# Projections for gates, queries, keys and values, emitted as steps inside the latent attention instead of as a block behind it

## The chip, the cores and the metric

The kernel runs on one core of a Trainium2 chip. The metric is the device time of one execution in microseconds (us). The profile is one execution, recorded by the hardware profiler; its times are counted from the first instruction. Engine names are those of the profile: PE is the matrix engine (PEld its weight loads), DVE the vector engine, ACT the scalar engine, POOL the GpSimd engine, SP the engine that issues most DMAs.

## What is computed

Two transformer blocks follow each other on 512 tokens of width 1024 in float32. The first ends in a mixture of sixteen experts; its weights are most of what is read. The change is in the second block, of which this is the core:

```python
h = rmsnorm_2(x, norm_g) * (1 + scale) + shift
ckv, kr, kb, vb, cq, za, qb, zb, ga, gb = split_cols(h @ w_in, KV_SPLITS + Q_SPLITS)
qa, ka, va = latent(cq, ckv, kr)             # 8 heads, 64 + 32 rotary columns, 256 more context rows
oa = block_attention(qa, ka, va, mla_scale)                       # the latent attention
ob = neighborhood_attention(qb, kb, vb, ctx_kb, ctx_vb, rpb)      # the near attention
ya = (oa * silu(za)) @ w_oa
yb = (ob * silu(zb)) @ w_ob
y = (sigmoid(ga) * ya + sigmoid(gb) * yb) @ w_out
x = x + gate * y
```

So the products of `h` with the columns for `za`, `ga`, `gb`, `qb`, `kb` and `vb` need only `h`. The latent attention doesn't need them, and the near attention doesn't need `oa`.

## The kernel before

The kernel is written in a tile framework. A tile names a pool and a tag; the tag has a fixed number of buffers, and a new tile of a tag waits until one is free. The framework places the instructions itself, with a timeline that it computes while it compiles: on each engine, of the instructions that are ready by this timeline, the one that was emitted earlier goes first. The order that results is fixed; on the chip every engine runs its own list from the front, and an instruction that waits holds those behind it.

A product of float32 operands is made from a high and a low part of each operand (`mm3`, lines 133 to 136: three matmuls). Weights come through `WStream` (line 188), one 512 KB block after the other in a fixed order: a DMA on SP, a copy to the high part on ACT (line 233), and the subtraction that gives the low part on DVE or POOL (line 234). There are two buffers for raw blocks (`P3W`) and six for parts (`P3H`), and two blocks, four part buffers, are one pair of 256 output columns.

The work around the change, by its name in the code:

- `latent()` (from line 1674): four pairs of heads, each in two halves of 256 queries, so eight units. A unit has six steps, one for each 128 keys. A step is `scores` (six matmuls and an exponential on ACT, psum tag `sc`), the next piece of `first` for the unit that follows (keys, transposed queries, and `peak`, the score maxima, which DVE reduces from tag `mx`), and `pv` of the step before. A unit ends with `close`: sums, a reciprocal on DVE and the output `oaT`. `first` of the first unit runs ahead of all.
- The projections, called fills below: `gate_fill` (silu gate `za`, letter A: four tiles of psum), `gates` (G10 and G00, two tiles each), `tok_fill` (Q and V, four each) and `keys_b` (K, two). They are called behind `latent()` in the order `MORD` = A G10 Q K G00 V. One tile takes 24 matmuls of 512 columns or 48 of 256. A gate tile leaves psum by a tanh on ACT (line 1657) and a product on DVE (line 1658), for A; the others by ACT alone.
- psum: `MPS` gives `sc` 2 buffers, `mx` 1, `po` 1 and `fl` 1. The fills take the first `NFL` = 5 tiles from `fl`, then `fl`, `sc`, `sc` in turn. Of 18 tiles 10 are `fl` and 8 are `sc`.
- `zaT`, where A's tiles go, is a tile of tag `b8` in pool `p3m`, with three buffers. It is requested behind `latent()`, in which pairs 1 and 3 request their transposed queries `qT` of the same tag.
- Behind the fills: the pools of the latent attention close, and `near()` opens its own. `key_turn` (line 1831 and following) turns the keys, `voff` takes shifted copies of `vb` by DMA (lines 1818 and 1819), and `near()` runs 16 units. Its own fills, `NORD` (more gates, and `out_proj`), are emitted behind it.
- `Filler` (line 285) takes generators and a credit in us: `pull(us)` adds credit and runs steps while it is positive, and each step takes off what it yields.

Of the kernel before, what the change touches and what calls it, by code (L numbers as in the profile page):

```python
# [9 lines left out]
F32 = mybir.dt.float32  # L10
# [3 lines left out]
AF = mybir.ActivationFunctionType  # L14
# [18 lines left out]
P1P=dict(ps=4,pp=2)  # L33
FO=[6,5,7,8,4]
PB2=6
NFL=5
PXE=1
NW_=9
NP=4
# [38 lines left out]
def body(ctx, tc, a, stop=None, dump=None):  # L78
# [44 lines left out]
    def ps(shape=(128, 512), dt=F32, tag="ps"):  # L123
        if tag == "fx":
            tag = next(fills)
        if tag == "tn":
            return ptn.tile(list(shape), dt, name=nm("ps"), tag=tag, bufs=2)
        return PS["pool"].tile(list(shape), dt, name=nm("ps"), tag=tag, bufs=PS[tag])
# [13 lines left out]
    def tsl(t):  # L142
        return slice(t * 128, (t + 1) * 128)
# [248 lines left out]
    def feat_block(w, m, act, p):  # L392
        for k in range(8):
            mm3(p, w(k, tsl(m)), act(k), k == 0, k == 7)
# [1240 lines left out]
    oaT = []  # L1635
    vb = p3m("b8", [128, 4, 512], F32, "vb")

    def tok_fill(x0, dst, scale=1.0, tag="fx"):
        for i in range(2):
            w = w3.pair(x0 + 2 * i)  # L1640
            for t0, nt, p in tok_block(w, 256, hT, tag=tag):
                c = slice(256 * i, 256 * i + 256)
                if isinstance(dst, list):
                    for t in range(nt):
                        S.activation(dst[t0 + t][:, c], p[:, t], AF.Copy, scale=scale)
                else:
                    S.activation(dst[:, t0:t0 + nt, c], p, AF.Copy, scale=scale)
                w3.ahead(x0 + 2 * i + 2 + t0 // 2)

    def gate_fill(x0, z, tag="fl"):  # L1650

        for m in range(4):
            p = ps(tag=tag)
            feat_block(w3.pair(x0 + 2 * (m // 2)), m % 2, hT, p)
            w3.ahead(x0 + m + 2)
            zm = z(m)
            S.activation(zm, p, AF.Tanh, scale=0.5)
            V.scalar_tensor_tensor(zm, zm, 1.0, p, op0=OP.add, op1=OP.mult)
# [3 lines left out]
    def gates(v, tiles, tag):  # L1662

        w = w3.pair(X_G[v])
        sgs[v] = []
        for m in range(2):
            p = ps(tag=tag)
            feat_block(w, m, hT, p)
            w3.ahead(X_G[v] + m + 2)
            g = tiles()  # L1670
            S.activation(g, p, AF.Tanh, scale=0.5)
            sgs[v].append(g)

    def latent():
# [93 lines left out]

        units = [(pr, f) for pr in range(4) for f in range(2)]
        for _ in first(0, 0):  # L1770
            pass
        for n, u in enumerate(units):
            g = first(*units[n + 1]) if n < 7 else iter(())
            for j in range(6):
                scores(*u, j)
                next(g, 0)
                if j:
                    pv(*u, j - 1)
            pv(*u, 5)
            for _ in g:  # L1780
                pass
            close(*u)

    psum(**MPS)
    latent()
    room = iter([x[:, t, 512:] for t in range(4)])
    zaT = p3m("b8", [128, 4, 512], F32, "zT")
    for v in MORD.split():
        if v == "K":
            keys_b(1, X["K"], "fx")  # L1790
        elif v == "Q":
            tok_fill(X["Q"], qb, 0.125)
        elif v == "V":
            tok_fill(X["V"], vb)
        elif v == "A":
            gate_fill(X["A"], lambda m: zaT[:, m], "fx")
        else:
            gates((int(v[1]), int(v[2])), lambda: next(room), "fx")
    for m in range(4):
        G.tensor_mul(oaT[m], oaT[m], zaT[:, m])  # L1800
    if stop == "oa":
# [155 lines left out]
    zbT = []  # L1957
    for v in NORD.split():
        if v == "B":
            gate_fill(X["B"], lambda m: zbT.append(p3m("b3", [128, 512], F32, "zT")) or zbT[m])  # L1960
        elif v[0] == "O":
            out_proj(int(v[1]), 0, "fl")
        else:
            gates((int(v[1]), int(v[2])), lambda: (next(room, None) if v != "G21" else None) or p3m("b2", [128, 512], F32, "sg"), "fl")
    if stop == "ob":
        dump("ob", obT.rearrange("p a b -> p (a b)"))
        for i in range(4):
# [21 lines left out]
    ymT = HL(pf, "b8", 4, 8, 512, "ymT")  # L1989
    for i in range(4):  # L1990
        if i == GI:
            gates((3, 1), lambda: p3m("b3", [128, 512], F32, "sg"), "pp")
        out_proj(i, 1, "pp")
        sg = sgs[i, 0] + sgs[i, 1]
        for m in range(2):
            G.tensor_add(sg[m], sg[m], sg[2 + m])
            src = sg[m].rearrange("p (b r c) -> p b r c", r=8, c=8)
            d = [v.rearrange("p (r b c) -> p b r c", r=8, c=8) for v in ymT(2 * i + m)]
            evac_hl(d[0], d[1], src)
        if i == 1:  # L2000
            nc.sync.dma_start(x, xd)
# [148 lines left out]
```

## Time and profile before

| What | us |
| --- | --- |
| median of three runs | 1945.97 (1945.35 to 1950.58) |
| the profiled execution | 1938.7 |
| its span, first to last instruction | 1936.9 |
| latent attention, from its first fill tile to its last sums | 1446 to 1604 |
| fills alone on PE | 1604 to 1675 |
| near attention with its fills | 1675 to 1843 |
| end of the block | 1843 to 1937 |

In the views below a busy time is the sum of an engine's instructions; PE's matmuls overlap, so neighbours in the list start sooner than the busy time of one says. PEclk is the granted clock of PE as a share of the full 2.4 GHz, so that 0.50 is 1.2 GHz. A bracket behind a row of the timeline is the time for which the engine stood idle before it, and what ended that.

### The profile page before, as it was taken

To read this page: it belongs to the slowest core of one execution; us is meant where nothing else is said; L and a number is where in the kernel's file an instruction comes from. 1 tells how busy PE (TensorE), PEld (TensorE's weight loads), DVE (VectorE), ACT (ScalarE), POOL (GpSimd) and SP (SyncE) were. 2 spreads that over 40 slices of the span, in tenths; PEclk is the share of its full clock that TensorE was granted. 3 is DMA by queue.
4 is the path that set the end of the run, shared out by engine and by line. 5 is a ranking of instruction groups with operands and counts; after the bars stand their busy time and mean duration, and the time that the engine had idled before them with its cause. 6 is when DMAs were issued, how large, how long until landed. Compare 5 with 4: busy or idle time off the path is not lost.

```text
span 1936.9 us, 24224 instructions
## 1 busy us (share of the span) xinstructions
PE 1751.3 (90%) x10016; PEld 1066.7 (55%) x10016; DVE 699.8 (36%) x1404; ACT 480.3 (25%) x929; POOL 246.6 (13%) x275
## 2 busy tenths in 40 slices
PE   6998999989999888988989888888899999999998
PEld 5984579963343232422323233322585669888878
DVE  6696786540111101001020010200556642354565
ACT  4335534421000000000000000000653432344433
POOL 2371201000000000000000000000031113223351
PEclk9999999999999999999999999999998999999999
DMA  6323513559999999999999999999420023432232
GB/s 213 109 80 103 190 51 98 206 230 420 425 426 426 426 425 427 426 426 426 426 426 426 426 425 426 425 427 425 144 81 12 1 66 96 103 99 81 87 109 88
DMA packets 96334, 500.47 MB, mean 258 GB/s; under 512 B 6628, under 2 KB 56640, under 8 KB 67808
## 3 DMA queue, kind: packets, MB, share of 16 engines
q1 hardware_dynamic: 90656, 479.06, 62.1%
q0 software_dynamic: 3696, 12.98, 2.0%
q10 hardware_dynamic: 1872, 6.88, 0.9%
q8 instruction: 79, 1.29, 0.3%
q14 instruction: 31, 0.25, 0.0%
HBM read 491.13 MB, written 6.72 MB: 257 GB/s over the span
## 4 chain that ended last, share of the span: by engine, by line
PE 48%; DMA 39%; DVE 6%; ACT 3%; POOL 2%; issue 2%; SPq 0%; DVEq 0%; ACTq 0%; POOLq 0%
DMA we<-in_expert_w_dram 37%; PE ps L131 24%; PE ps L134 7%; PE ps L135 7%; PE ps L136 7%; DMA w<-in_ca_wkv_dram 1%; DMA w<-in_w_out_dram 1%; DVE wl L234 1%; PE ps L1902 1%; ACT wh L233 1%; PE ps L752 1%; POOL wl L234 1%; DVE qkc L530 1%; DMA voff<-vb 1%; POOL sq L462 0%
## 5 line engine op out<-in xcount | busy, mean ns | idle before, releaser
L131 PE MATMUL ps<-we,xe 128*64 128x512 f32 x2048 | 464.8, 602 | 59.6 <-DMA we<-in_expert_w_dram 59.6
L131 PEld LDWEIGHTS ps<-we,xe 128*64 128x64 f32 x2048 | 144.3, 138 | 354.7 <-issue 263.7
L131 PE MATMUL ps<-we,hT 128*64 128x512 f32 x1024 | 233.2, 598 | 28.2 <-DMA we<-in_expert_w_dram 21.6
L131 PEld LDWEIGHTS ps<-we,hT 128*64 128x64 f32 x1024 | 69.8, 136 | 161.5 <-issue 128.3
L233 ACT ACTIVATE wh<-w 128x1024 fp32r<-128x1024 f32 (+4 forms) x100 | 104.0, 1042 | 141.9 <-PE ps L135 94.2
L1307 DVE TENSOR_TENSOR hid<-hid,ps 128x512 f32<-128x512 f32 x32 | 22.0, 688 | 321.8 <-PE ps L131 300.4
L1349 DVE SCALAR_TENSOR_TENSOR y<-ps,gate,y 64x512 fp32r<-64x512 f32 x32 | 24.0, 749 | 311.6 <-ACT y L1348 311.6
L1315 ACT ACTIVATE hT<-ps 128x512 f32<-128x512 f32 x32 | 19.1, 597 | 424.3 <-PE ps L1313 424.3
L305 POOL DMA_DIRECT2D gg<-in_rows_dram x2 | 1.1, 548 | 903.9 <-PE ps L131 903.9
L234 DVE TENSOR_TENSOR wl<-w,wh 128x1024 fp32r<-128x1024 f32 (+4 forms) x62 | 82.5, 1333 | 90.4 <-ACT wh L233 90.1
L234 POOL TENSOR_TENSOR wl<-w,wh 128x1024 fp32r<-128x1024 f32 (+1 forms) x34 | 81.9, 2413 | 198.0 <-ACT wh L233 197.9
L1348 ACT ACTIVATE y<-ps,gate 64x512 fp32r<-64x512 f32 x32 | 21.8, 682 | 259.3 <-PE ps L131 246.2
L134 PE MATMUL ps<-hTh,wh 128*128 128x512 f32 x192 | 76.5, 399 | 1.7 <-ACT va L1631 1.7
L135 PE MATMUL ps<-hTl,wh 128*128 128x512 f32 x192 | 76.0, 396 | 0.0
L136 PE MATMUL ps<-hTh,wl 128*128 128x512 f32 x192 | 75.8, 397 | 0.0
L131 PEld LDWEIGHTS ps<-otT,xn 128*128 128x128 f32 x512 | 60.7, 195 | 24.0 <-issue 21.9
L131 PE MATMUL ps<-otT,xn 128*128 128x128 f32 x512 | 66.3, 285 | 1.0 <-ACT otT L1254 1.0
L135 PE MATMUL ps<-wl,hTh 128*128 128x256 f32 (+1 forms) x224 | 66.2, 296 | 0.0
L134 PE MATMUL ps<-wh,hTh 128*128 128x256 f32 (+1 forms) x224 | 66.2, 297 | 0.0
L136 PE MATMUL ps<-wh,hTl 128*128 128x256 f32 (+1 forms) x224 | 64.9, 295 | 0.0
L1266 DVE TENSOR_TENSOR xe<-ps,cols 128x512 f32<-128x512 f32 (+1 forms) x18 | 10.2, 599 | 145.9 <-PE ps L131 145.9
L1306 ACT ACTIVATE hid<-ps 128x512 f32<-128x512 f32 x32 | 19.1, 596 | 158.7 <-PE ps L131 158.7
(571 smaller groups left out, 3330.6 us busy)
## 6 DMA issues: line engine op xcount, KB each, us to landing
we<-in_expert_w_dram SPq DMA_DIRECT2D x171, 2048.0 KB, 34.3
we<-in_expert_w_dram SPq DMA_DIRECT2D x42, 1024.0 KB, 34.3
w<-in_w_in_dram SPq DMA_DIRECT2D x48, 512.0 KB, 3.7
w<-in_w_mod_dram SPq DMA_DIRECT2D x24, 512.0 KB, 4.3
w<-in_w_out_dram SPq DMA_DIRECT2D x16, 512.0 KB, 3.7
w<-in_ca_wkv_dram SPq DMA_DIRECT2D x8, 512.0 KB, 4.3
wcv<-in_ctx_kv_dram SPq DMA_DIRECT2D x2, 2048.0 KB, 21.7
bm<-in_bias_dram POOLq DMA_DIRECT2D x16, 256.0 KB, 3.0
```

The source lines that it names most:

```text
L131: T.matmul(out, l, r, start=st, stop=sp)
L134: T.matmul(out, L[0], R[0], start=st, stop=False)
L135: T.matmul(out, L[0], R[1], start=False, stop=False)
L136: T.matmul(out, L[1], R[0], start=False, stop=sp)
L233: S.activation(h, w, AF.Copy)
L234: (G if (self.ns % 3 == 2 if self is ws else W3E(self.ns)) else V).tensor_sub(l, w, h.bitcast(F32))
L530: V.scalar_tensor_tensor(o, u[:, 6 + j:518 + j], conv(m, j), o, op0=OP.mult, op1=OP.add)
L752: T.transpose(pp[:, j], st[u][hf][:, tsl(j)], ident)
L1307: V.tensor_mul(h, h, pu)
L1348: S.activation(Y[q][r, 2 * d], p[r], AF.Copy, scale=g)
L1349: V.scalar_tensor_tensor(Y[q][r, 2 * d + 1], p[r], g, Y[q][r, 2 * d].bitcast(F32), op0=OP.mult, op1=OP.subtract)
L1902: T.transpose(p[:, j], st[u][i][:, tsl(j)], ident)
```

## The change

The fills become generators. `tok_part` yields after every four of a tile's k (12 matmuls of 256 columns), `feat_part` after every two (6 of 512 columns), each time 1.4. K is now a case of `tok_fill`. They are handed to a `Filler` before `latent()` starts; `first` of the first unit pulls `FS` = 1.5 after each of its pieces, every step of a unit pulls `FJ` = 2.0 behind its scores, and what is left is drained behind `latent()`. `zaT` is requested before `latent()`. `NFL` becomes 14. The same functions, used behind the near attention, are run to their end at once by `steps_of`.

```diff
-NFL=5
+NFL=14
+FS=1.5
+FJ=2.0
...
+    def tok_part(w, p, t, n):
+        for k in range(8):
+            mm3(p[:, n:n + 256], hT(k, tsl(t)), w(k), k == 0, k == 7)
+            if k % 4 == 3:
+                yield 1.4
+
+    def feat_part(w, m, p):
+        for k in range(8):
+            mm3(p, w(k, tsl(m)), hT(k), k == 0, k == 7)
+            if k % 2:
+                yield 1.4
...
+    def tok_fill(x0, dst, scale=1.0, n=2):
+        for i in range(n):
             w = w3.pair(x0 + 2 * i)
+            for t in (0, 2):
+                p = ps(tag="fx")
+                for j in range(2):
+                    yield from tok_part(w, p, t + j, 256 * j)
+                for d, s in dst(i, t, p.rearrange("p (t n) -> p t n", t=2)):
+                    S.activation(d, s, AF.Copy, scale=scale)
+                w3.ahead(x0 + 2 * i + 2 + t // 2)
...
         for _ in first(0, 0):
-            pass
+            fill.pull(FS)
         for n, u in enumerate(units):
             g = first(*units[n + 1]) if n < 7 else iter(())
             for j in range(6):
                 scores(*u, j)
+                fill.pull(FJ)
                 next(g, 0)
                 if j:
                     pv(*u, j - 1)
             pv(*u, 5)
             for _ in g:
-                pass
+                fill.pull(1)
             close(*u)
...
     psum(**MPS)
-    latent()
     room = iter([x[:, t, 512:] for t in range(4)])
     zaT = p3m("b8", [128, 4, 512], F32, "zT")
...
+    fill = Filler(*(fills_of(v) for v in MORD.split()))
+    latent()
+    fill.drain()
```

## Rows read from the trace of the kernel before

**Rows 1.** The page's first part: busy time, share of the span, instructions.
```profile
PE 1751.3 (90%) x10016; PEld 1066.7 (55%) x10016; DVE 699.8 (36%) x1404; ACT 480.3 (25%) x929; POOL 246.6 (13%) x275
```

**Rows 2.** Busy times by stage; stretch, length, engines (instructions), PEclk, DMA share, GB/s.
```profile
1444.00:1452.00 8.00, 6.34 (x32) 5.02 (x31) 3.90 (x8) 2.88 (x6) 7.56 (x8) 1.00 0.08 26
1452.00:1460.00 8.00, 4.71 (x19) 2.43 (x18) 4.90 (x7) 1.45 (x4) 3.93 (x5) 0.79 0.24 66
1460.00:1475.00 15.00, 15.00 (x59) 9.69 (x59) 5.65 (x8) 5.25 (x9) 0.00 (x0) 0.54 0.00 0
1475.00:1517.00 42.00, 40.43 (x267) 25.66 (x268) 33.94 (x48) 18.64 (x36) 8.00 (x9) 1.00 0.00 1
1517.00:1528.00 11.00, 8.96 (x42) 5.96 (x38) 6.28 (x9) 2.67 (x5) 3.25 (x4) 0.70 0.01 1
1528.00:1542.00 14.00, 13.41 (x89) 8.48 (x86) 11.08 (x16) 7.24 (x15) 1.27 (x1) 0.99 0.01 2
1542.00:1555.00 13.00, 13.00 (x70) 8.47 (x70) 5.83 (x9) 4.21 (x7) 3.50 (x3) 1.00 0.27 86
1555.00:1563.00 8.00, 5.13 (x19) 3.79 (x18) 5.91 (x7) 1.43 (x3) 1.28 (x1) 0.79 0.41 122
1563.00:1604.00 41.00, 40.12 (x224) 28.09 (x223) 16.26 (x20) 12.63 (x19) 3.64 (x2) 1.00 0.09 26
1604.00:1675.00 71.00, 71.00 (x548) 68.91 (x548) 15.16 (x22) 23.67 (x37) 23.05 (x16) 1.00 0.36 99
1675.00:1703.00 28.00, 26.27 (x140) 22.01 (x139) 15.87 (x24) 11.73 (x20) 6.96 (x6) 1.00 0.47 113
1703.00:1843.00 140.00, 139.78 (x930) 112.41 (x930) 70.40 (x127) 60.04 (x123) 47.53 (x47) 1.00 0.29 89
```

**Rows 3.** PE's timeline, 1445 to 1456: start, length, line, operation, idle time before.
```profile
1445.93 0.50 PE L134 MATMUL ps<-hTh,wh 128*128 128x512 f32 x1 [1.66 <-ACT va L1631]
...
1451.52 0.40 PE L136 MATMUL ps<-hTh,wl 128*128 128x512 f32 x1
...
1453.64 0.59 PE L131 MATMUL ps<-kT,qT 96*128 96x512 f32 x2 [1.14 <-POOL kT L1689]
...
1455.37 0.59 PE L131 MATMUL ps<-kT,qT 96*128 96x512 f32 x2 [1.14 <-DVE mx L1710]
```

**Rows 4.** ACT's and DVE's timelines where A's first tile leaves psum.
```profile
1538.74 0.59 ACT L1657 ACTIVATE zT<-ps 128x512 f32<-128x512 f32 x1
...
1536.93 1.76 DVE L1752 RECIPROCAL rs<-ps 128x256 f32<-128x256 f32 x1 [0.19 <-PE ps L131]
...
1539.85 0.67 DVE L1658 SCALAR_TENSOR_TENSOR zT<-zT,ps 128x512 f32<-128x512 f32 x1
```

**Rows 5.** PE's timeline from A's second tile to its third.
```profile
1542.68 0.39 PE L134 MATMUL ps<-hTh,wh 128*128 128x512 f32 x1
...
1553.72 0.40 PE L136 MATMUL ps<-hTh,wl 128*128 128x512 f32 x1
...
1558.76 0.38 PE L131 MATMUL ps<-cst,mx 128*2 128x128 f32 x2 [2.87 <-DVE mx L1710]
...
1559.88 0.63 PE L134 MATMUL ps<-hTh,wh 128*128 128x512 f32 x1
```

**Rows 6.** DVE's timeline in the gap between those two tiles.
```profile
1556.15 1.75 DVE L1752 RECIPROCAL rs<-ps 128x256 f32<-128x256 f32 x1
...
1558.63 0.67 DVE L1658 SCALAR_TENSOR_TENSOR zT<-zT,ps 128x512 f32<-128x512 f32 x1
```

**Rows 7.** DVE's timeline where the latent attention ends and the near one prepares.
```profile
1603.88 1.76 DVE L1752 RECIPROCAL rs<-ps 128x256 f32<-128x256 f32 x1 [0.74 <-PE ps L131]
...
1609.49 1.43 DVE L1831 COPY tk<-x 128x512 f32<-128x512 f32 x4
```

**Rows 8.** The chain that ended last, 1676 to 1687: start, length, what.
```profile
1676.55 10.01 DMA voff<-vb
```

**Rows 9.** PE's timeline, 1675 to 1703, its only idle time over 0.2 us.
```profile
1689.39 1.27 PE L1834 MATMUL ps<-cst,tk 128*128 128x128 f32 x8 [1.73 <-DVE kc L1836]
```

More of the change, by code (lines that the diff above doesn't have):

```diff
@@ L1636, in body, with steps_of @@
     vb = p3m("b8", [128, 4, 512], F32, "vb")
-    def tok_fill(x0, dst, scale=1.0, tag="fx"):
-        for i in range(2):
-            w = w3.pair(x0 + 2 * i)
[L1641 to L1648, printed above, removed]
+    def steps_of(gen):
+        for _ in gen:
+            pass
+    def tok_part(w, p, t, n):
[10 more added lines that the diff above has]
+        for i in range(n):
+            w = w3.pair(x0 + 2 * i)
+            for t in (0, 2):
[5 more added lines that the diff above has]
+                w3.ahead(x0 + 2 * i + 2 + t // 2)
     def gate_fill(x0, z, tag="fl"):
         for m in range(4):
+            w = w3.pair(x0 + 2 * (m // 2))
             p = ps(tag=tag)
-            feat_block(w3.pair(x0 + 2 * (m // 2)), m % 2, hT, p)
+            yield from feat_part(w, m % 2, p)
             w3.ahead(x0 + m + 2)
@@ L1667, in gates @@
             p = ps(tag=tag)
-            feat_block(w, m, hT, p)
+            yield from feat_part(w, m, p)
             w3.ahead(X_G[v] + m + 2)
@@ L1780, in latent, with fills_of @@
             for _ in g:
-                pass
+                fill.pull(1)
             close(*u)
     psum(**MPS)
-    latent()
     room = iter([x[:, t, 512:] for t in range(4)])
     zaT = p3m("b8", [128, 4, 512], F32, "zT")
-    for v in MORD.split():
+    def fills_of(v):
         if v == "K":
[L1790 to L1798, printed above, removed]
+            return tok_fill(X["K"], lambda i, t, p: [(kb[:, t:t + 2, 4:8], p.rearrange("p t (h d) -> p t h d", h=4))], n=1)
+        if v == "Q":
+            return tok_fill(X["Q"], lambda i, t, p: [(qb[t + j][:, 256 * i:256 * i + 256], p[:, j]) for j in range(2)],
+                            0.125)
+        if v == "V":
+            return tok_fill(X["V"], lambda i, t, p: [(vb[:, t:t + 2, 256 * i:256 * i + 256], p)])
+        if v == "A":
+            return gate_fill(X["A"], lambda m: zaT[:, m], "fx")
+        return gates((int(v[1]), int(v[2])), lambda: next(room), "fx")
+    fill = Filler(*(fills_of(v) for v in MORD.split()))
+    latent()
+    fill.drain()
     for m in range(4):
@@ L1959, in body @@
         if v == "B":
-            gate_fill(X["B"], lambda m: zbT.append(p3m("b3", [128, 512], F32, "zT")) or zbT[m])
+            steps_of(gate_fill(X["B"], lambda m: zbT.append(p3m("b3", [128, 512], F32, "zT")) or zbT[m]))
         elif v[0] == "O":
@@ L1963, in body @@
         else:
-            gates((int(v[1]), int(v[2])), lambda: (next(room, None) if v != "G21" else None) or p3m("b2", [128, 512], F32, "sg"), "fl")
+            steps_of(gates((int(v[1]), int(v[2])), lambda: (next(room, None) if v != "G21" else None) or p3m("b2", [128, 512], F32, "sg"), "fl"))
     if stop == "ob":
@@ L1991, in body @@
         if i == GI:
-            gates((3, 1), lambda: p3m("b3", [128, 512], F32, "sg"), "pp")
+            steps_of(gates((3, 1), lambda: p3m("b3", [128, 512], F32, "sg"), "pp"))
         out_proj(i, 1, "pp")
```

## The prediction, made before the changed kernel ran

> **What bounds the kernel now.** I read the page's first part first: PE is busy for 1751.3 us, 90% of the span, and no other engine passes 36% [rows 1]. So the kernel as a whole is paced by PE and, in the experts, by what PE waits for there; the change touches neither the experts nor the number of matmuls. What it can win is time in which PE stands still or runs at the low clock, in the stretch that it rearranges. That is why the second view is the table by stage [rows 2]: for each stretch the reader takes length minus PE's busy time (idle), and length times (1 minus PEclk) (lost to the clock).
>
> Idle, from 1444 to 1604: 1.66 + 3.29 + 0 + 1.57 + 2.04 + 0.59 + 0 + 2.87 + 0.88 = 12.9 us. Clock: 0.21 x 8 = 1.7, 0.46 x 15 = 6.9, 0.30 x 11 = 3.3, 0.01 x 14 = 0.1, 0.21 x 8 = 1.7, together 13.7 us; some of it falls on idle time (the idle shares of the three stretches that have both give 0.7 + 0.6 + 0.6), so 11.8 us count. From 1604 to 1675 PE is busy without a gap, from 1675 to 1703 it loses 1.7, from 1703 to 1843 only 0.2 [rows 2]. **The ceiling of the change is therefore 12.9 + 11.8 + 1.7 = 26.4 us**, 1.4% of the span; the 71 us of fills alone are no waste, since PE does useful work there.
>
> The third view, the timelines, says why the loss sits where it does. The planner already moves fills into the latent attention, and one can see it: A's first tile runs from 1445.93 to 1451.9, inside the preparation of the first unit [rows 3]. Then nothing follows for 87 us. Its tanh runs at 1538.74 [rows 4], though its matmuls were done at 1451.9 and ACT is busy for only 18.64 of 42 us [rows 2]. I read this as a wait for `zaT`: it is the last of the `b8` tiles requested, behind the `qT` of pairs 1 and 3, and pair 1 has just made its last sums (the reciprocal at 1536.93 is its) [rows 4]. While the tile waits, the one `fl` bank is taken and no fill can start. At 1542.68 the second tile starts [rows 5], and from there to 1604 fills and attention alternate. So the latent attention runs alone from 1452 to 1542, with DVE busy for 33.94 of 42 us [rows 2], and there PE has its low clock and most of its gaps.
>
> **The change, part by part.** *Instructions.* None is added or removed on any engine: the same 18 tiles, 8 weight pairs and evictions, so 0 us of work. *Weights.* Their DMAs on SP, the copies on ACT and the subtractions on DVE and POOL move with the fills. SP has nothing else here (DMA share 0.00 to 0.01 from 1460 to 1542), ACT and POOL have room; on DVE they meet a busy engine, but a step that now also holds 2 us of fill lasts about twice as long, so DVE's share falls from 0.81 towards half [rows 2]. I cost it at nothing; without that cover each subtraction on DVE would be one more queue ahead of a maximum, as in the gap below.
>
> *Credit.* `first` pulls 5 x 1.5, the 48 steps pull 48 x 2.0, together 103.5; the 18 tiles yield 18 x 5.6 = 100.8. So the last fill, V, ends in the last but one step of the last unit, and nothing is left to drain. The yield of 5.6 a tile fits: 12 tiles take 71 us with some transposes among them [rows 2].
>
> *`zaT` first.* It now takes a `b8` buffer before `qT` of pair 1, and `qT` of pair 3 has to wait for pair 1 instead, which has ended two units before it is wanted. Cost 0; the 87 us for which a bank was held are gone.
>
> *Start, 1444 to 1460.* Idle now 1.66 + 3.29 = 4.95. The 1.66 (the bank is freed by an eviction on ACT) and the 1.14 before 1453.64 (POOL) [rows 3] stay; the gaps at the maxima are filled by A's second tile, once the first has left psum. I keep 3.0 idle, a gain of 2.0; bounds 0 and 3.3. The low clock follows these gaps: 4.71 busy of 8, then 0.54 for 15 us, while 1.73 idle in 28 us [rows 9] and 0.88 in 41 left it at 1.00 [rows 2]. With the gaps halved I take it as not falling: gain 1.0 + 6.9 = 7.9, rounded to 8, bounds 0 and 8.
>
> *The seven and a half units that follow, 1475 to 1604.* Lost now: idle 7.95, clock 3.9 (of the 11.8), together 11.9. What the interleaved regime loses is shown by its own rows, and they lie apart: 0.88 in 41 us, or, with the gap at 1558.76 and its clock, 2.87 + 0.88 + 1.1 = 4.9 in 62 us (1542 to 1604) [rows 2]. The regime will last about 200 us: the attention's own work is 160 us (1444 to 1604) less the 24.7 lost and less six tiles of fills at 5.6, so 102, and the fills are 101. That gives 4.3 or 15.8 us. The gap arises because a maximum stands behind a 1.75 us reciprocal and a subtraction on DVE [rows 5, 6], when the planner has put the maxima at the seam of two units; with a fill behind every score they have time to come in their own steps. I take 7, nearer to the first: gain 5, bounds -4 and 8.
>
> *The single bank.* 16 of 18 tiles now share `fl`, instead of 10. A tile's bank was free again only 2.0 to 5.8 us after its last matmul (from 1554.1 to 1559.88 in [rows 5], with its DVE product at 1558.63 [rows 6]), and PE must have attention work for that long. It has about 102/18 = 5.7 us for each tile, with two banks for scores, so I cost it at 0 beyond the term above; the third rival has the other end.
>
> *Start of the near attention.* What the 71 us of fills covered comes to stand bare: from the last reciprocal to the end of the key copies 1603.88 to 1610.92, 7.0 us on DVE [rows 7]. What covers it now are the first two tiles of the next gates, 11.2 us of PE, but only if their psum is free. The 10.01 us DMA from `vb` [rows 8] and the gap of 1.73 that comes with it [rows 9] stay late in any order, or come some us sooner, since V ends a step before the attention. Extra cost between -1.7 and 7.0; I take 3, nearer to the covered end. The stretch from 1703 on is full and keeps its length [rows 2].
>
> Sum: 2 + 8 + 5 - 3 = 12 us. The profiled execution would go from 1936.9 to 1925 of span; the median lies 7.3 above the profiled execution's 1938.7 and keeps that distance, so 1946 - 12 = **1934 us**.
>
> **Rivals.** *First, the clock still falls at the start and the near attention starts bare:* 2 + 0 + 5 - 7 = 0 to 2 + 0 + 5 - 3 = 4, so 1942 to 1946. For it: the bank of the first tile and POOL's copies are not touched by the change, and 1517 to 1528 shows a fall after only 2.04 us idle [rows 2].
>
> *Second, nearly all comes back:* 3.3 + 8 + 8 + 1.7 = 21, so 1925. For it: 41 us of the same regime with 0.88 idle [rows 2].
>
> *Third, slower: the bank sets the pace.* PE's list is in order, so a fill placed by the planner before its bank is really free stops scores too. One such turn cost 2.87 + 1.1 = 4.0 us at 1555 to 1563 [rows 2, 5]. Against a ceiling of 26.4 with 3 left at the start and 3 added at the near one, five bad turns of 16 leave nothing of the gain that can be measured; at nine it is 36 - 20 = 16 slower, 1962. Against it: of four turns in 1542 to 1604 one was bad.
>
> The Trainium skill, "TensorE: Matmul & The Clock Gate", section "A second HAM failure mode: psum-queue depth-cycling", speaks against this change: cycling through psum banks makes PE idle briefly between groups of matmuls, often enough that its clock swings between its levels. By that rule this third rival would be the likely one; the trace agrees only once, with PEclk 0.79 at 1555 to 1563, and shows 1.00 over the next 41 us.
>
> *Fourth, the change does not do what it says:* only the move of `zaT` and the planner matter, and steps by hand give what the planner would have given. The time would be that of the forecast, 1934, and its chance lies inside the forecast's; it is a question of cause.
>
> **How the numbers follow.** Chances: forecast 0.46 (1928 to 1938), second rival 0.16, first rival 0.25, third 0.13. A measurement of this kernel can tell about 0.3%, 5.8 us, from no change. Forecast and second rival are faster, 0.62; the first is within, 0.25; the third is slower, 0.13. The range goes from 1922 (the ceiling less 2) to 1950, 4 above the first rival, for the units' term nearer to its lower bound; the third rival and a little on either side stay out.
>
> **What would show it.** Right: A's first tanh within 5 us of its last matmul; no stretch of 0.5 clock between 1455 and 1475; fill matmuls between the scores of all eight units; V's last eviction at the last unit; the first near scores some 10 us sooner than at 1703. Wrong: PE idle ended by ACT or by DVE's `zT` at the turns of the tiles (third rival); PE idle of over 5 us behind the last sums (first); a clock below 1.00 at the seams of the units.

## The result and the profile after

The changed kernel takes **1919.28 us** (median of 4 runs, 1918.83 to 1920.45), the kernel before 1945.66 us in the same measurement (4 runs, 1944.06 to 1950.58). The ratio is 0.9861, with a 95% interval of 0.9843 to 0.9879: 1.4% faster, 26.4 us where 12 were forecast. Its profiled execution took 1919.15 us, its span is 1917.4 us. Against the profiled execution of before, span to span, that is 19.5 us. So the missed 14.4 us are two misses of about the same size: 7.5 in the sum, and 6.9 in the distance between the profiled execution and the median.

The page's first part of the changed kernel; PE was busy for 1751.3 us before [rows 1].

```profile
PE 1739.1 (91%) x10016; PEld 1062.0 (55%) x10016; DVE 702.1 (37%) x1404; ACT 478.4 (25%) x929; POOL 248.0 (13%) x275
```

The number of matmuls is the same, and PE is busy for 12.2 us less: it did the same work at the high clock for longer. The table by stage of the changed kernel (stretch, length, busy time of PE, PEld, DVE, ACT and POOL with the number of instructions, PEclk, DMA share, GB/s), to be held against [rows 2]:

```profile
1444.00:1452.00 8.00, 8.00 (x39) 6.56 (x38) 6.14 (x12) 4.36 (x8) 7.61 (x13) 1.00 0.25 68
1452.00:1465.00 13.00, 11.09 (x51) 7.53 (x50) 6.51 (x11) 4.37 (x8) 8.55 (x7) 1.00 0.30 81
1465.00:1512.00 47.00, 46.19 (x254) 32.75 (x253) 26.52 (x33) 17.45 (x29) 4.17 (x3) 1.00 0.17 45
1512.00:1530.00 18.00, 17.65 (x128) 14.46 (x127) 8.84 (x14) 7.14 (x15) 5.50 (x5) 1.00 0.11 30
1530.00:1654.00 124.00, 123.69 (x877) 98.75 (x875) 57.37 (x72) 45.76 (x78) 25.17 (x17) 1.00 0.21 60
1654.00:1692.00 38.00, 36.15 (x186) 30.47 (x185) 27.91 (x45) 14.34 (x26) 14.14 (x15) 0.96 0.39 101
1692.00:1823.00 131.00, 131.00 (x878) 105.81 (x876) 66.32 (x121) 58.09 (x120) 49.53 (x46) 1.00 0.29 87
```

Length minus PE's busy time gives 0 + 1.91 + 0.81 + 0.35 + 0.31 + 1.85 + 0 = 5.2 us idle, and only one stretch has a clock below 1.00: 0.04 x 36.15 = 1.4 us. That is 6.7 us lost where before lost 26.4 by the same reading. PE's timeline has only seven places from 1444 to 1823 at which it waited for 0.25 us or more (start, length, operation, in brackets the idle time before it and what ended it); the last row is one of the slower matmuls behind the seventh:

```profile
1454.05 0.59 PE L133 MATMUL ps<-kT,qT 96*128 96x512 f32 x2 [1.14 <-DVE mx L1730]
1461.69 0.61 PE L133 MATMUL ps<-kT,qT 96*128 96x512 f32 x2 [0.39 <-DVE mx L1730]
1463.48 0.38 PE L133 MATMUL ps<-cst,mx 128*2 128x128 f32 x2 [0.25 <-DVE mx L1730]
1490.48 0.65 PE L133 MATMUL ps<-P,va 128*64 128x256 f32 x4 [0.32 <-ACT P L1752]
1511.90 0.38 PE L133 MATMUL ps<-cst,mx 128*2 128x128 f32 x2 [0.49 <-DVE mx L1730]
1512.63 0.39 PE L136 MATMUL ps<-wh,hTh 128*128 128x256 f32 x1 [0.35 <-ACT x L1691]
...
1656.04 0.50 PE L136 MATMUL ps<-hTh,wh 128*128 128x512 f32 x1 [1.85 <-DVE rs L1772]
...
1657.20 0.63 PE L137 MATMUL ps<-hTl,wh 128*128 128x512 f32 x1
```

The largest wait has moved to the end: the near attention's first gate tile waits for the last reciprocal, and behind that wait the matmuls of 512 columns take 0.63 us instead of 0.40, the half clock, until 1660.2. ACT's timeline answers [rows 4]: the tanh of A's first tile runs half a microsecond after the start of the tile's last matmul (1451.94), not 87 us later; V's last eviction and the first exponential of the near attention follow.

```profile
1452.42 0.60 ACT L1677 ACTIVATE zT<-ps 128x512 f32<-128x512 f32 x1 [0.83 <-PE ps L138]
...
1646.33 0.59 ACT L1666 ACTIVATE vb<-ps 128x512 f32<-128x512 f32 x1
...
1691.72 0.69 ACT L1918 ACTIVATE P<-ps,mx 128x512 f32<-128x512 f32 x1 [4.57 <-DVE mx L1916]
```

In the kernel before the first of these exponentials ran at 1704.30: 12.6 us of the gain are there by then, and the other 5.5 by the near attention's last output, because 22 of its stretch's matmuls now stand ahead of it.

### The profile page after: what moved, and what is told of

The parts are those of the page before. It is cut to its first block, busy times and chain, and to the rows that moved or that the text cites. A ratio compares the mean times of both kernels' runs of the same rounds, so it can differ in the third digit from the quotient of the medians.

```text
span 1917.4 us, 24223 instructions
## 1 busy us (share of the span) xinstructions
PE 1739.1 (91%) x10016; PEld 1062.0 (55%) x10016; DVE 702.1 (37%) x1404; ACT 478.4 (25%) x929; POOL 248.0 (13%) x275
## 4 chain that ended last, share of the span: by engine, by line
PE 52%; DMA 39%; DVE 5%; ACT 2%; issue 1%; POOL 1%; SPq 0%; ACTq 0%; DVEq 0%; POOLq 0%
DMA we<-in_expert_w_dram 37%; PE ps L133 24%; PE ps L136 8%; PE ps L137 8%; PE ps L138 8%; DMA w<-in_ca_wkv_dram 1%; PE ps L1927 1%; PE ps L754 1%; DVE wl L236 1%; DVE qkc L532 1%; DMA w<-in_w_out_dram 1%; POOL sq L464 0%; ACT wh L235 0%; PE ps L1503 0%; PE ps L260 0%
```

## The experiments

Five questions: what frees the tiles, whether one bank is enough, what it costs the attention to stand alone, what could still be had at the start of the near attention, and why the median moved further than the profile. "Lost" is idle time of PE plus its busy time times (1 minus PEclk), in the stretch named. The runs were made in five groups, each with the kernel before on the same chip. The times are medians; the ratio is taken from all executions of both kernels and not from the two medians, whose quotient would be 0.9912 for e9 and 0.9905 for e10.

| run | us | before beside it | ratio (95%) |
|---|---|---|---|
| e1, before again | 1945.92 | 1942.55 | 0.9997 (0.9974 to 1.0021) |
| e2, steps, nothing pulled | 1953.43 | 1942.55 | 1.0059 (1.0034 to 1.0084) |
| e3, `zaT` touched, 5 in `fl` | 1935.48 | 1942.55 | 0.9954 (0.9926 to 0.9982) |
| e4, `zaT` touched, 14 in `fl` | 1925.19 | 1942.55 | 0.9914 (0.9890 to 0.9938) |
| e5, after again | 1920.62 | 1945.22 | 0.9872 (0.9855 to 0.9888) |
| e6, after, banks shared | 1919.71 | 1945.22 | 0.9868 (0.9851 to 0.9884) |
| e7, after, fills in 4 units | 1918.66 | 1945.22 | 0.9864 (0.9848 to 0.9881) |
| e8, after, V ahead of G00 | 1923.57 | 1945.22 | 0.9883 (0.9867 to 0.9900) |
| e9, after, fills in 2 units | 1924.37 | 1941.44 | 0.9881 (0.9817 to 0.9944) |
| e10, after, one tile left over | 1922.90 | 1941.44 | 0.9867 (0.9804 to 0.9930) |
| e11, before, close late | 1944.12 | 1943.22 | 1.0028 (1.0006 to 1.0049) |
| e12, e3 with close late | 1928.22 | 1943.22 | 0.9926 (0.9900 to 0.9952) |
| e13, after, third time | 1919.37 | 1944.64 | 0.9873 (0.9848 to 0.9898) |
| e14, e4 again | 1925.20 | 1944.64 | 0.9902 (0.9879 to 0.9925) |

### What frees the tiles

The prediction read the 87 us for which A's first tile held the one `fl` bank as a wait for pair 1's end. The lists that the framework makes say something else: with the request of `zaT` alone moved ahead of `latent()`, they are the same as those of the kernel before, so that would be the same kernel. A tile of `b8` gets its buffer in the order of the instructions that first *write* the tag's tiles. In the kernel before the tanh that first writes `zaT` is emitted behind all of the attention, so it stands behind the first write of pair 3's `qT`. ACT's timeline of the kernel before shows just these two, one behind the other:

```profile
1538.48 0.37 ACT L139 ACTIVATE qT<-ps 96x256 fp32r<-96x256 f32 x1
1538.74 0.59 ACT L1657 ACTIVATE zT<-ps 128x512 f32<-128x512 f32 x1
```

(The reciprocal at 1536.93 in [rows 4], which the prediction gave to pair 1, is the fifth unit's, pair 2's first half.) Three kernels tell the readings apart. The first is the changed kernel with nothing pulled, so that the request stands early and the steps are all emitted behind the attention:

```diff
-FS=1.5
-FJ=2.0
+FS=0
+FJ=0
```

> The changed kernel with both credits 0: the fills are generators, zaT is requested first and 14 tiles go to fl, but all steps are drained behind the attention. If the request of zaT is what frees the fills, as the prediction had it: 1920 to 1935. If zaT gets its buffer only by the order in which instructions first write the tiles of its tag, nothing is freed (PE's list then has one fill tile up to the fifth unit's sums, as the kernel before): 1943 to 1949. Both say that the number of fl tiles alone does nothing.

The other two are the kernel before with `zaT` requested and one column of it written ahead of `latent()`, without any steps; e4 has `NFL=14` as well, as the changed kernel has.

```diff
 psum(**MPS)
+zaT = p3m("b8", [128, 4, 512], F32, "zT")
+V.memset(zaT[:, 0, 0:1], 0.0)
 latent()
 room = iter([x[:, t, 512:] for t in range(4)])
-zaT = p3m("b8", [128, 4, 512], F32, "zT")
```

> The kernel before, its fills in one piece behind the attention and 5 tiles in fl, but zaT is requested ahead of the attention and written there by one memset of one column. If the order of first writes is what held A's first tile, the planner now moves fills by itself: its list for PE has 3.8 tiles at the first unit's sums, 6.2 at the third's, and then none until the attention's end, since the next tiles want sc. The losses of the start and of the first three units go (start 3 + 8, a third of the units' 12), the others stay: 1930 to 1934. If emission between the steps is what counts, 1943 to 1949.

> As the last, with 14 tiles in fl. No fill is emitted between steps; the planner's list has 3.8, 5.0, 7.0, 8.4, 10.0, 11.0, 13.8 and 15.0 tiles at the eight units' sums and three behind the attention. If the hold by zaT and the wait for sc are the whole cause, it takes what the change takes, 1917 to 1922, and the three tiles left cover the start of the near attention. If emission in steps has a worth of its own, 1925 to 1940.

With the request early and nothing pulled the hold is there as before: the first tile's last matmul starts at 1456.76, and its tanh runs at 1543.98, again right behind a `qT`. The single write takes it away: in e3 the tanh runs at 1457.07. ACT's timelines of e2 and of e3:

```profile
1543.72 0.37 ACT L141 ACTIVATE qT<-ps 96x256 fp32r<-96x256 f32 x1
1543.98 0.59 ACT L1677 ACTIVATE zT<-ps 128x512 f32<-128x512 f32 x1
```

```profile
1457.07 0.60 ACT L1657 ACTIVATE zT<-ps 128x512 f32<-128x512 f32 x1 [0.83 <-PE ps L136]
```

So the first write is the cause of the hold, shown by taking it away. e2 at 1953.43 us lies above both of its ranges, slower than the kernel before, and its timeline says where: PE idles for 9.9 us from the last sums to the near attention's first exponential, where e1, the kernel before, idles for 1.7. Behind the attention the fills run bare, now through one bank, and six tiles wait for the one ahead of them to be evicted, with idle times of 1.40, 0.75, 1.35, 0.53, 1.40 and 0.69 us (two more waits, 1.08 and 0.60, are for weights). Two of the six:

```profile
1611.60 0.39 PE L136 MATMUL ps<-wh,hTh 128*128 128x256 f32 x1 [1.40 <-ACT x L1691]
...
1625.96 0.39 PE L136 MATMUL ps<-wh,hTh 128*128 128x256 f32 x1 [1.35 <-ACT qb L1666]
```

That is the third rival's mechanism, with its price: 6.1 us for six turns where nothing else stands between two tiles.

How far does one column written early go? In e3 six tiles are made early, and then the tiles of tag `sc` wait for the attention's scores to end. In e4 15 of 18 come early, and the ratio is 0.9914. e3's 1935.48 us lies 1.5 above its range, and e4's 1925.19 at the near end of the range for steps with a worth of their own. Run beside the changed kernel on one chip, in more executions:

> The touched kernel with 14 tiles in the fl bank, unaltered (zaT touched ahead of the attention, no steps), now beside the changed kernel on one chip. In profiled executions it stood 3.6 us above the changed kernel between the attention's start and the near attention's last output, with as little idle. Theory (the steps are worth those 3.6 us, and the rest of the distance between the two ratios, 0.9914 to 0.9867, was the chip's): 3 to 5.5 us slower than the changed kernel. Rival (the steps are worth the whole distance): 7 to 11 us slower.

e14 takes 1925.20 us (6 runs, 1920.42 to 1929.72) and e13, the changed kernel, 1919.37: 5.8 us apart, between the theory's 3 to 5.5 and the rival's 7 to 11, and nearer to the theory. So by the medians, of 25.3 us beside the kernel before, 19.4 come from letting the planner move the tiles, with one write and `NFL`, and about 6 from the steps. The windows of e14 (the first unit, then the other seven) show that the units have nothing left to win: 0.18 us idle in 152 us, at full clock.

```profile
1444.00:1486.73 42.73, 39.31 (x193) 27.37 (x194) 21.76 (x33) 16.01 (x27) 13.46 (x13) 1.00 0.14 39
1486.73:1639.05 152.32, 152.14 (x995) 114.74 (x996) 77.65 (x99) 55.34 (x97) 32.89 (x24) 1.00 0.17 49
```

From the first fill tile to the near attention's last output, the profiled executions take 378.3 us (after), 381.9 (e4) and 379.9 (e14). What e14's other executions lose to the changed kernel's is not settled.

### Is one bank enough?

The changed kernel with only the first 5 tiles kept to `fl`, the others in `fl`, `sc`, `sc` in turn:

```diff
-NFL=14
+NFL=5
```

> The changed kernel with only the first 5 of its 18 filling tiles in the fl bank, the others in the two banks of the scores, as before the change. The third rival of the prediction (the one fl bank sets the pace in the changed kernel): the tiles get a second bank, and it is faster than the changed kernel by 3 us or more. Theory now (the change wins because the filling never stops, and the one bank is hidden by the attention's work between two steps): no faster; a half-made tile now holds a score bank through some ten steps, which leaves the attention one bank for its scores, so 3 to 20 us slower than the changed kernel, with idle of TensorE ahead of score matmuls.

1919.71 us, 0.9 less than the changed kernel on that chip; the executions overlap (1918.37 to 1920.97, and 1919.91 to 1921.35). Neither expectation was right: the third rival's 3 us are not there, nor is the loss of 3 to 20 us to half-made tiles in score banks. The near attention's start loses less in e6 (0.65 and 0.49 us idle in place of 1.85, the clock at 1.00), and the stretch as a whole no less: 378.7 us by the same reading as above. Banks don't set the pace here, in either division.

### What does it cost the attention to stand alone?

The first theory behind the result was that the attention loses time wherever nothing stands between its steps. e7 and e9 are the changed kernel with more pulled at each step, so that all tiles are made beside the first four units, or the first two:

```diff
-FJ=2.0
+FJ=4.0
```

> The changed kernel with twice as much pulled at each of the attention's steps (FJ 4 in place of 2): the same instructions, but all 18 tiles are made by the end of the fourth of eight units and the last four units stand alone. Theory (what the change gives back is lost wherever attention stands alone: in the kernel before 1512 to 1604, which is mostly the last four units, TensorE idled 6.4 us and the clock cost about 4): 8 to 14 us slower than the changed kernel, the idle and the half clock now in the last four units, none of it in the first four. Rival (it is the start of the attention alone, with the clock's fall there, and the order of the first writes that cost): as fast as the changed kernel within 3 us.

```diff
-FJ=2.0
+FJ=8.0
```

> The changed kernel with 8 pulled at each step (FJ 8 in place of 2): all 18 filling tiles are made beside the first two units, and six units stand alone, among them every later change of pair. Theory now (attention that stands alone costs only 0.3 to 0.8 us a unit, as in units 2 to 4 of the kernel before; what is dear is a single place, where DVE's list has the reciprocal of one unit right ahead of the maxima mx that the next unit's queries wait for: TensorE waits 1.9 us there and its clock falls for 3 to 9 us' worth; before has this at the end of unit 4, the touched kernel with 5 tiles at the end of unit 6): this kernel's list has that order at the ends of units 3, 5 and 6, all alone now, so waits of 1.9 us at two or three of them and at least one fall of the clock, 5 to 14 us slower than the changed kernel (1924 to 1933 beside 1919 to 1921). Rival (only the start of the attention mattered; with 18 tiles made early enough nothing is lost later): within 3 us of the changed kernel.

e7 is as fast as the changed kernel (1918.66 beside 1920.62, with ratios whose intervals overlap): the theory fell. The windows of e7, first unit, units 2 to 4 with the fills, and units 5 to 8 alone:

```profile
1444.00:1484.46 40.46, 38.56 (x198) 27.94 (x196) 21.50 (x32) 17.07 (x27) 14.62 (x14) 1.00 0.18 51
1484.46:1602.91 118.45, 118.45 (x831) 100.72 (x830) 45.55 (x55) 40.02 (x66) 27.65 (x17) 1.00 0.23 65
1602.91:1651.76 48.85, 46.27 (x305) 29.51 (x304) 35.80 (x50) 21.15 (x39) 7.63 (x8) 1.00 0.09 31
```

Four units alone lose 2.6 us, and the clock stays. In e9 it is six units, and the loss is the same 2.6; the 4.1 us of idle in its second unit, which holds 14 tiles, are mostly two waits of 1.05 for maxima, one of 1.08 and one of 0.60 for weights, and one of 0.33 at the bank. e9 lies at the near end of its range of 1924 to 1933, but not for the reason given there: no wait of 1.9 us, and no fall of the clock in the units. The windows of e9, its second unit and units 3 to 8:

```profile
1486.59:1588.20 101.61, 97.49 (x681) 86.30 (x680) 25.06 (x32) 30.60 (x50) 20.77 (x14) 1.00 0.24 69
1588.20:1658.00 69.80, 67.22 (x454) 44.45 (x454) 53.97 (x72) 30.27 (x56) 12.86 (x12) 1.00 0.10 31
```

e3, with units 4 to 8 alone, is another matter. Its sixth unit ends with the order that cost the kernel before 2.04 us at 1517 to 1528 [rows 2]: reciprocal, then the maximum for which PE waits. There PE idles 1.90 us and the clock falls to 0.67 for a unit, 2.4 and 6.1 us lost:

```profile
1571.01:1592.01 21.00, 18.62 (x83) 11.50 (x84) 10.33 (x14) 5.15 (x9) 1.26 (x1) 0.67 0.08 31
```

But the same order on DVE stands at three seams of e9 (1599.87, 1624.35, 1636.33) and costs nothing there. DVE and PE at the seam of the kernel before at 1517.64, then at the first of those three in e9:

```profile
1517.64 1.76 DVE L1752 RECIPROCAL rs<-ps 128x256 f32<-128x256 f32 x1 [0.19 <-PE ps L131]
1519.31 0.90 DVE L1710 TENSOR_REDUCE mx<-ps 128x1 f32<-128x768 f32 x1
1520.27 0.38 PE L131 MATMUL ps<-cst,mx 128*2 128x128 f32 x2 [1.90 <-DVE mx L1710]
```

```profile
1599.87 1.74 DVE L1772 RECIPROCAL rs<-ps 128x256 f32<-128x256 f32 x1
1601.53 0.89 DVE L1730 TENSOR_REDUCE mx<-ps 128x1 f32<-128x768 f32 x1
1601.26 2.66 PE L133 MATMUL ps<-qT,kT 98*128 98x256 f32 x18
1603.85 0.38 PE L133 MATMUL ps<-cst,mx 128*2 128x128 f32 x2
```

In e9 PE's list has 18 score matmuls, 2.66 us, ahead of the matmuls that need the maximum; in the kernel before it has nothing there. In the changed kernel two seams have the order as well: at 1611.22 fill matmuls run until 1614.94 and PE doesn't wait, at 1509.28 it waits 0.49 us.

The second theory, which e11 and e12 try, was that the order on DVE is what is dear. They take it away in the kernel before and in e3, by writing each unit's close behind the first scores of the next unit:

```diff
             for j in range(6):
                 scores(*u, j)
+                if j == 0 and n:
+                    close(*units[n - 1])
                 next(g, 0)
...
-            pv(*u, 5)
             for _ in g:
                 pass
-            close(*u)
+            pv(*u, 5)
+        close(*units[7])
```

> The kernel before, with nothing filled in, but each unit's close (sums, reciprocal, output) written behind the first scores of the next unit instead of ahead of them; the same instructions. By the lists that the framework makes, DVE's reciprocal of 1.76 us then stands behind both maxima that the next unit's queries need, where in the kernel before it stands ahead of the second at the ends of units 4 and 6, with nothing else for TensorE to do in between. Theory (later in the attention the kernel before lost its time at these two places alone: 2.1 us idle and 3 to 9 us of clock in unit 5, 2.7 and 1.5 in unit 7, rows of the profiled executions): 5 to 12 us faster than the kernel before; what its start loses (5.1 idle, 7.4 clock) stays. Rival (a bare attention waits and loses its clock somewhere or other whatever the order): within 3 us of the kernel before.

> The touched kernel (zaT requested and touched ahead of the attention, 5 tiles in the fl bank, some 6 of 18 tiles made early, units 3 to 8 alone) with the close written late as well. Theory: the touched kernel's loss at the end of unit 6 (2.4 us idle and 6.1 of clock in unit 7) goes too, so about 8 us faster than the touched kernel, ratio 0.988 to 0.992 to the kernel before, with two thirds of the attention alone and nearly all of the change's gain; what then still separates it from the changed kernel is 1.5 to 5 us. Rival (filling beside the units is needed): as the touched kernel, 0.993 to 0.998.

e11 is 0.3% slower than the kernel before, at best the same: this theory fell too. The 1.9 us wait is gone, others, of 0.97, 0.68 and 0.44 us twice each and some smaller, came in its place from unit 2 on, and the clock fell in units 2 to 5, where the kernel before had its two places [rows 2]. The windows of e11, units 1 to 5:

```profile
1444.00:1480.63 36.63, 30.89 (x137) 20.18 (x136) 18.36 (x28) 12.85 (x23) 11.74 (x12) 0.77 0.07 22
1480.63:1496.92 16.29, 14.32 (x87) 9.10 (x87) 12.36 (x16) 5.59 (x12) 6.11 (x6) 0.93 0.00 1
1496.92:1511.68 14.76, 14.08 (x81) 10.03 (x82) 10.03 (x14) 6.12 (x11) 0.00 (x0) 0.85 0.01 2
1511.68:1528.14 16.46, 14.50 (x87) 9.29 (x87) 12.35 (x16) 5.59 (x12) 6.10 (x6) 0.91 0.00 1
1528.14:1546.33 18.19, 16.82 (x81) 11.06 (x82) 10.20 (x14) 6.12 (x11) 0.00 (x0) 0.70 0.00 0
```

e12's ratio of 0.9926 falls between its two ranges (0.988 to 0.992, 0.993 to 0.998). It lies 0.28% below e3, with intervals that overlap, and still loses the clock in units 4 and 5 (0.96 and 0.74). What holds over all of these: the clock's fall at the start (7.1 us in e11, 6.9 + 1.0 in [rows 2]) is gone in every kernel in which A's second tile stands between the first unit's maxima, e3, e4, e12 and e14, which have no steps, among them. Units that stand alone lose 0.6 us each in e7 and 0.4 in e9 on average, and in e11 units 2 to 5 lose 6.0 us idle and 9.5 of clock. Which it is depends on the order that the framework makes, and not on the place of the reciprocal alone: the seams above say that PE waits where its own list has no other work ahead of what needs the maximum. No run moves that work alone, so for e11's waits and for the clock this stays open.

### The start of the near attention

The 1.85 us before G11 and the half clock behind it are the changed kernel's largest loss. Two kernels try to leave a tile there. e8 makes the values ahead of G00, and pulls less; e10 only pulls less:

```diff
-MORD='A G10 Q K G00 V'
-FJ=2.0
+MORD='A G10 Q K V G00'
+FJ=1.7
```

> The changed kernel with the values made ahead of the gates G00 (the order A G10 Q K V G00 for A G10 Q K G00 V) and 1.7 pulled for 2.0, so that about one tile of G00 is left when the last unit ends and V, which the shift of values across the halves (voff) waits for, is out earlier. Theory (the changed kernel's loss at the start of the near attention, 1.85 us idle ahead of the first gate tile G11 and 1.5 us of half clock after it, comes from having no filling left there, and a tile of G00 covers it): 2 to 4 us faster than the changed kernel. Rival (the wait passes to the query copies, as the 1.73 us of rows 9, or the lower pull costs in the units what it saves here): the same within 2 us.

```diff
-FJ=2.0
+FJ=1.7
```

> The changed kernel with 1.7 pulled for 2.0 in the old order A G10 Q K G00 V: about one tile of V, 7 us of matmuls, is left when the last unit ends, and stands ahead of G11 and the near attention's first transposes. Theory (the 1.85 us of idle and 1.5 us of half clock at G11 have no cover, and any tile left gives it): 1 to 3.5 us faster than the changed kernel. Rival (the wait passes on to the token copies tk or to the shifted values voff, which come later by as much, as with the values ahead, where TensorE waited 3.39 us for tk): the same within 1, or up to 4 us slower.

Neither is faster. In e8 G11 no longer waits, but the first transposes of the near attention do, 3.39 us for the token copies on DVE, with the half clock behind them, and the median is 3 us above the changed kernel's on that chip. In e10 they wait 1.54 us until V's last tile is evicted; its ratio of 0.9867 is about the changed kernel's, and the wide interval allows no more than that. The wait moves on to what is late next, as the rivals had it. PE's timelines of e8 and e10:

```profile
1659.81 1.29 PE L1859 MATMUL ps<-cst,tk 128*128 128x128 f32 x8 [3.39 <-DVE tk L1856]
```

```profile
1658.17 1.53 PE L1859 MATMUL ps<-cst,tk 128*128 128x128 f32 x12 [1.54 <-ACT vb L1666]
```

No kernel here beats the changed one by more than the measurement can tell; e7 comes nearest, with all four executions (1918.21 to 1919.66) below the changed kernel's four on that chip.

### Why the median moved further than the profile

> The kernel before, unchanged, profiled a second time. The first profile (1938.7 us) was 7 us quicker than the median of the timed executions (1945.97). If the low clock of PE in the attention that runs alone is longer in a usual execution, the second profile reads about 1945 and has its extra time between the first fill tile and the last sums (158 us in the first profile: 1446 to 1604). If the experts' weight loads vary, the extra lies before the first fill tile (1446 us in the first profile). Median of the timed executions 1944 to 1948 by both.

> The changed kernel once more, unaltered, so that the next three can be set beside it on one chip, and so that its own spread is seen beside that of the kernel before. Theory 1 (a part of the kernel before's spread lies in the stretch of attention that stood alone, where one profiled execution lost 11.8 us to the clock and another, 11.6 us longer, about 19): with that stretch gone the executions of the changed kernel lie within 6 us of each other, while those of the kernel before spread over 10 or more; ratio 0.984 to 0.988. Theory 2 (the spread comes from the chip as a whole, the same in both): both spread alike, by 10 us or more.

> The changed kernel, unaltered, in more executions, beside the next one on the same chip. The prediction took the distance of 7.3 us between the kernel before's profiled execution and its median for one that the change leaves; in the changed kernel it was 0.1. Theory 1 (the distance lies in the stretch of attention alone and goes with it): all executions of the changed kernel within 6 us. Theory 2 (it lies ahead of the attention, as 4.6 of the 11.6 us between two profiled executions of the kernel before did, and comes and goes with the chip): some executions of the changed kernel stand 5 us or more above the fastest, too.

e1 is the kernel before, unaltered, and its profiled execution has a span of 1948.5 us, 11.6 more than the first one. Two stretches of the kernel before's first profile, then the same two of e1: up to the first fill tile, and from there to the near attention's first exponential.

```profile
0.00:1445.93 1445.93, 1284.99 (x7058) 691.28 (x7058) 447.53 (x1010) 299.11 (x600) 106.55 (x161) 0.99 0.79 321
1445.93:1704.30 258.37, 245.41 (x1491) 189.55 (x1492) 124.15 (x174) 89.90 (x152) 61.32 (x51) 0.95 0.20 54
```

```profile
0.00:1450.53 1450.53, 1292.96 (x7058) 697.30 (x7059) 447.71 (x1010) 299.34 (x600) 106.07 (x161) 0.98 0.79 320
1450.53:1714.62 264.09, 251.24 (x1491) 192.84 (x1492) 123.87 (x174) 89.89 (x153) 61.33 (x51) 0.92 0.19 53
```

4.6 us lie ahead of the attention, 5.7 in it and 1.3 behind; the expectation had the extra time in one place or the other, and it is in both. The 4.6 come with a fall of the clock from 240 to 260 us, 0.26 x 19.32 = 5.0 us by the reading above, here in the first profile and in e1:

```profile
240.00:260.00 20.00, 19.12 (x117) 11.86 (x119) 18.70 (x59) 9.09 (x23) 2.81 (x9) 1.00 0.25 80
```

```profile
240.00:260.00 20.00, 19.32 (x88) 11.26 (x88) 14.83 (x48) 6.11 (x15) 2.61 (x8) 0.74 0.23 80
```

Of the sixteen profiles e2 and e3 show this fall too, and the others don't; e2 is built from the changed kernel, so the fall doesn't hang on the change. The 5.7 are one place, the fifth unit, in the first profile and in e1:

```profile
1517.64:1536.93 19.29, 17.16 (x88) 10.61 (x88) 12.12 (x16) 6.71 (x13) 2.61 (x4) 0.82 0.00 1
```

```profile
1522.30:1547.32 25.02, 22.98 (x89) 13.92 (x89) 12.12 (x16) 6.77 (x13) 2.60 (x4) 0.59 0.00 1
```

The idle time is the same, 2.1 and 2.0 us, and the clock is 0.82 and 0.59. So the same program paid 3.1 us of clock for that one wait in one execution and 9.4 in another, and the first profile was a cheap execution in both places. (e2 has the same unit with the same wait, at 0.82.) How the 6.9 us divide between the two falls is not shown, since only profiled executions show where the clock fell. The changed kernel's 13 executions of the first measurement, e5 and e13 lie between 1918.69 and 1922.57, within the 6 us of the first theory; the kernel before's 4, 7 and 11 beside them between 1937.79 and 1951.02. But the theory is not the whole: e14, which has no unit alone and in its profiled execution no clock below 1.00 in the units, scatters over 9.3 us; e12, whose units 4 and 5 fall to 0.96 and 0.74, only over 1.2 in four executions. Why none of the changed kernel's 13 executions is longer by the 4.6 us that e1 lost ahead of the attention, in work that the change doesn't touch, stays open.

## Why the prediction was wrong, point by point

The direction, the mechanism and the place were right; the time was below the range. By the terms of the sum, in profiled executions:

| term | predicted | measured |
|---|---|---|
| start, idle | 2 | 4.95 - 1.91 = 3.0 |
| start, clock | 8 | 7.9 |
| the units | 5 | 11.9 - 1.47 = 10.4 |
| start of the near attention | -3 | 1.73 - 1.85 - 1.4 = -1.5 |
| sum | 12 | 19.8 (spans: 19.5) |
| profile to median | 0 | 6.9 |

**The units' term was mis-sized, 5.4 us.** The prediction priced the interleaved attention from 1542 to 1604 of the kernel before and took a value between 0.88 us in 41 and 4.9 in 62. The changed kernel loses 0.81 + 0.35 + 0.31 = 1.47 us in 189. The step that failed is the choice of 7 us lost, for the gap that arises "when the planner has put the maxima at the seam of two units": the 2.87 us at 1558.76 [rows 5] were read as a feature of interleaving, and they were the price of a seam at which PE's list had no other work ahead of what needs the maximum. In the changed kernel DVE's order of reciprocal and maximum still stands at two seams, and PE waits 0.49 us at one and not at all at the other, so even the upper bound of 8 was too low. The sentence that a fill behind every score gives the maxima time agrees with these rows; e7 and e9 show that scores alone can do the same.

**The distance to the median was the other half, 6.9 us.** "Keeps that distance" had no row behind it. One profiled execution stood 7.3 us under its median. Two falls of the clock that it had cheaply or not at all can make that up: the price of one wait (3.1 us there, 9.4 in e1), which the change removes, and the fall at 240 to 260 us, which the change does not touch. How much of the 6.9 us each has is open. That the medians lie 26.4 us apart, as many as the ceiling, is chance: by the profiles 19.7 of those 26.4 came back. A stretch with a fallen clock should have been read as a cost that varies, and a second profile of the same kernel would have shown it.

**The start was right in size, by other waits than it named.** It gave back 7.9 of 8 us of clock, and 3.0 of idle, within the bounds. The two waits that were to stay, 1.66 us at the bank and 1.14 for POOL, are gone; what stayed is the 1.14 at the second peak (1454.05, for a maximum), which was to be filled. That the idle came out near is in part luck. **The near attention's start** cost 1.5 in place of 3, for the reason given: two gate tiles cover it once their psum is free, and that is the 1.85 us.

**The reading of `zaT` was wrong in its cause and right in its effect.** It does not wait for pair 1's end; the request's place changes nothing, the first write's does (e2, e3). The prediction's sentence that the earlier request frees the bank would have been false without the steps, which bring the first write forward.

**The rivals.** The second, nearly all comes back, was the one that happened, at 0.16: its 21 us are the 19.8 of the profiled executions, and with the distance kept it was priced at 1925, 5.7 too slow. The first (clock still falls, near attention bare) did not happen: the clock is 1.00 until 1654. The third's mechanism exists, and e2 gives its price, 6.1 us for six turns of a bare bank. In the changed kernel one turn shows, 0.35 us at 1512.63, since the attention's work stands between two tiles; e6 with shared banks is no faster. The Trainium skill, "TensorE: Matmul & The Clock Gate", section "A second HAM failure mode: psum-queue depth-cycling", tells of a kernel that cycles through psum banks and idles briefly between groups of matmuls, so often that the clock swings. By that this rival would have been the likely one; the changed kernel's trace does not agree, with 16 of 18 tiles in turn through one bank and PEclk 1.00 from 1444 to 1654. The fourth, a question of cause, was three quarters right: one column written early and `NFL`, without steps, give 19.4 of 25.3 us on one chip (e13, e14).

**The signs.** Right: the first tanh 0.5 us behind the start of its last matmul, fill matmuls in all eight units (in the last until 1645.21), no half clock from 1455 to 1475, V's last eviction in the last unit (1646.33, the last reciprocal at 1654.22), DVE's share down to 26.52 / 47 = 0.56 from 1465 to 1512. The near attention's first exponential came 12.6 us sooner; for its scores some 10 were expected.

## What to carry to other kernels

When a tile holds a scarce bank for long, look at the order in which its buffer's tag is first written, not at where the tile is requested; one early write can be worth more than a rewrite of the loop. Price waits at a seam as a property of the order that the framework made for that emission, on the engine that is late and on the one that waits, and look at what the new emission does to both before carrying them over. And take a second profile of the kernel before, if a stretch at the low clock is part of the sum: its cost varies from execution to execution.

## What the runs showed of the hardware that was not expected

The same wait in the same instructions, 1.9 us of idle at the start of the fifth unit, cost 3.1 us of clock in one execution and 9.4 in another (unit clock 0.82 and 0.59), so the length of the stretch at the lower of the two levels, 1.2 GHz, is not fixed by the program. Nor does the length of a wait alone decide: e2 waits 1.90 us at 1525.52 and its unit falls to 0.82, and it waits 2.02 us at 1705.19 and keeps 2.4 GHz; in e11 the clock falls behind waits of 0.97 and 0.44 us at 1492.42 and 1493.29 and stands at 1.2 GHz from 1496 to 1500, the start of unit 3. In e9 units 3 to 8 idle 2.6 us in 70, in pieces of at most 0.69, and keep 2.4 GHz. A reciprocal of 128 x 256 elements took 1.76 us on DVE, beside 0.41 for a product of the same shape; that is what stands ahead of a maximum at a seam.
